# Seven-product gate/up tiles in all four feed-forward blocks instead of two

## The chip, the cores and the metric

The kernel runs on one core of a Trainium2 chip. The metric is the device time of one execution in microseconds (us); lower is better.

## The reference

The program is one inference step of a two-layer decoder for 512 prompt tokens and 64 sample tokens (576 in all, `D_MODEL` 1024), which share their weights. Layer 0 mixes tokens by a recurrence (RWKV-7), layer 1 by dilated window attention. Each layer has a feed-forward block before its mixer and one after it, so that there are four in all. What matters here, cut from the reference:

```python
def swiglu(x, wi, wo):
    gate, up = jnp.split(x @ wi, 2, axis=-1)      # wi: 1024 x 5632, wo: 2816 x 1024
    return (jax.nn.silu(gate) * up) @ wo

h = h + 0.5 * swiglu(rms_norm(h, w['norm_w'][i, 0]), w['ffn1_wi'][i], w['ffn1_wo'][i])
# ... mixer of layer i ...
h = h + 0.5 * swiglu(rms_norm(h, w['norm_w'][i, 2]), w['ffn2_wi'][i], w['ffn2_wo'][i])
h = h + jax.nn.sigmoid(rms_norm(h, w['norm_w'][i, 3]) @ w['pe_gate'][i]) * (p[i] @ w['pe_proj'][i])
```

Between the layers there is also a shared key/value projection, and layer 1 needs a table of position biases.

## The kernel before

Features lie on the 128 partitions and the 576 tokens on the free axis. A matmul streams half of the tokens (288 columns, `HF`) against one 128x128 weight tile. Each float32 operand is split into a high part H (a float32r cast by ACT) and a low part L (the value minus H, by DVE or POOL). A product of two operands is three matmuls, H·H, H·L and L·H. Weights come in pieces of 256 KB on SP's queue (`load_w`, line 166, buffers `wr`); ACT casts them (line 169) and POOL subtracts (line 170).

A feed-forward block (`ffn`) has 22 pairs of a gate tile and an up tile, each of 128 features by 576 tokens, and then the second product with `wo`. Two forms of a pair exist:

- **The standard pair** (`pair`, lines 359 to 373) takes 2 tiles x 8 inner tiles x 3 x 2 halves = 96 matmuls. Its inputs are the split activations `x`. DVE evicts the gate halves (line 365), ACT applies Silu, POOL multiplies by the norm's factor `rs` (line 368), and DVE evicts the up halves (line 371). Then the result `u` is split into two `hv` buffers (lines 154 and 155).
- **The seven-product pair** (`pair7`, lines 375 to 414) regards gate/up by token halves by inner halves as a 2x2 by 2x2 block product, and does it with seven block products (Strassen's scheme in Winograd's form). That is 7 x 4 inner tiles x 3 = 84 matmuls (line 390). Its weights are formed in `seven`: four loads into `wr` and `sr` (line 325), three sums on DVE into PSUM (line 337), one on POOL (line 346), and seven splits (lines 331 and 332). Its token sums are made once a block by `forms`.

`forms` returns five steps. Steps 0 to 3 are `sums(k)`: two normalised activations into two `hv` buffers (line 292), then four sums (lines 294 to 297), split into `TH` and `TL`. Step 4, `quarters`, splits the unsummed parts into the `x` buffers, which are then no longer needed as inputs of standard pairs.

With `fast` given, a block does the first five pairs (`F_STD`) in the standard form, calls step j of `forms` behind pair j, and does the other 17 pairs with seven products. Pair 4 goes through its inner tiles in the outer loop, so that it holds four PSUM banks and releases the `x` buffers one by one. Only the first block of layer 0 ("f0") and the second of layer 1 ("f2") are built with `fast`. The two blocks between them, in phase "f1" (called "f1a" and "f1b" in this text), use 22 standard pairs, two parts of the second product with 11 tiles each, and 26 `hv` buffers. In f1a the three position-bias tables (`bias_table`, called by `mid` behind pairs 2, 5 and 8) are worked in.

The second product is cut into parts, so that `hv` buffers can be used again. A part of tiles a to b starts when pair b (one beyond its last) has been issued (lines 424 to 441).

The order of instructions on each engine's queue is fixed when the kernel is built: a list scheduler takes instructions by program order as priority, and by the times at which its model says that they are ready. On the chip each engine goes through its queue in that order, so that an instruction that waits holds up all those behind it on its engine. Tags such as `hv`, `u`, `t1`, `ev` and `ss` are pools of that many buffers; a new use waits until the last reader of an old one is done.

## Time and profile before

| | us |
|---|---|
| median of 3 runs (lowest to highest) | 2925.57 (2924.57 to 2925.61) |
| the profiled execution | 2930.93 |
| its span, first to last instruction | 2928.8 |
| busy: PE (matmul) | 2786.2, 95% |
| busy: PEld (weight load, beside PE) | 2604.7, 89% |
| busy: DVE / ACT / POOL | 1386.5 / 1198.0 / 1454.0 |

PE runs the matmuls; its busy time is near the span. The profile gives the granted TensorE clock as a share of full speed, 0.975 over the span. Of the blocks named above, f0 takes the time from 8 to 428 us of the span, f1a from 1106 to 1547, f1b from 1629 to 2049, and f2 from 2440 to 2858.

### The profile page before, as it was taken

To read this page: it belongs to the slowest core of one execution; us is meant where nothing else is said; L and a number is where in the kernel's file an instruction comes from. 1 tells how busy PE (TensorE), PEld (TensorE's weight loads), DVE (VectorE), ACT (ScalarE), POOL (GpSimd) and SP (SyncE) were. 2 spreads that over 40 slices of the span, in tenths; PEclk is the share of its full clock that TensorE was granted. 3 is DMA by queue.
4 is the path that set the end of the run, shared out by engine and by line. 5 is a ranking of instruction groups with operands and counts; after the bars stand their busy time and mean duration, and the time that the engine had idled before them with its cause. 6 is when DMAs were issued, how large, how long until landed. Compare 5 with 4: busy or idle time off the path is not lost.

```text
span 2928.8 us, 56127 instructions
## 1 busy us (share of the span) xinstructions
PE 2786.2 (95%) x22360; PEld 2604.7 (89%) x22360; DVE 1386.5 (47%) x2940; ACT 1198.0 (41%) x2296; POOL 1454.0 (50%) x1196
## 2 busy tenths in 40 slices
PE   7899988988999999999999999999999999899997
PEld 7899987977776778999999999999888879899997
DVE  5533338467667654211226321122577775524345
ACT  4434345443333224222335422233456655435354
POOL 6756557553323335444544454454544326757553
PEclk9999998999989899999999999999999999999999
DMA  3233233222113112222233322223433443233223
GB/s 120 81 91 91 87 111 127 70 57 64 44 43 79 40 50 73 85 82 85 83 91 103 96 82 84 83 86 108 131 84 98 132 147 105 80 88 94 87 78 103
DMA packets 177082, 257.81 MB, mean 88 GB/s; under 512 B 46889, under 2 KB 68849, under 8 KB 176820
## 3 DMA queue, kind: packets, MB, share of 16 engines
q1 hardware_dynamic: 148736, 223.56, 25.4%
q10 hardware_dynamic: 28084, 30.66, 3.8%
q8 instruction: 176, 2.88, 0.4%
q14 instruction: 86, 0.70, 0.1%
HBM read 234.31 MB, written 19.85 MB: 87 GB/s over the span
## 4 chain that ended last, share of the span: by engine, by line
PE 71%; DVE 9%; issue 3%; ACT 2%; POOL 2%; DMA 1%; ACTq 0%; DVEq 0%; SPq 0%; POOLq 0%
PE ps_e L196 39%; PE ps_d L517 10%; PE ps_e L390 6%; PE ps_i L517 2%; PE ps_q L517 2%; PE ps_s L517 2%; PE ps_w L517 2%; PE ps_x L517 1%; PE ps_o L517 1%; PE ps_d L390 1%; DVE AR L583 1%; PE ps_pt L526 1%; DVE S L1307 1%; PE ps_d L196 1%; PE ps_y L517 1%
## 5 line engine op out<-in xcount | busy, mean ns | idle before, releaser
L170 POOL TENSOR_TENSOR wl<-wr,wh 128x512 fp32r<-128x512 f32 (+2 forms) x613 | 777.2, 1272 | 975.8 <-ACT wh L169 926.7
L196 PE MATMUL ps_e<-x,wh 128*128 128x288 f32 x3968 | 797.3, 296 | 13.0 <-ACT x L261 7.9
L169 ACT CAST wh<-wr 128x512 fp32r<-128x512 f32 (+2 forms) x613 | 362.2, 594 | 931.7 <-PE ps_e L196 723.8
L196 PEld LDWEIGHTS ps_e<-x,wh 128*128 128x128 f32 x3968 | 639.6, 189 | 18.7 <-ACT x L261 7.9
L196 PE MATMUL ps_e<-hv,wh 128*128 128x288 f32 x2944 | 587.8, 295 | 3.2 <-POOL hv L155 1.9
L196 PE MATMUL ps_e<-x,wl 128*128 128x288 f32 x1984 | 586.5, 296 | 1.4 <-POOL wl L170 1.4
L196 PEld LDWEIGHTS ps_e<-hv,wh 128*128 128x128 f32 x2944 | 472.6, 188 | 4.1 <-POOL hv L155 2.4
L196 PE MATMUL ps_e<-hv,wl 128*128 128x288 f32 x1472 | 434.2, 295 | 1.2 <-POOL wl L170 1.2
L517 PE MATMUL ps_d<-x,wh 128*128 128x288 f32 x1664 | 370.9, 310 | 7.0 <-DVE q L1370 3.3
L196 PEld LDWEIGHTS ps_e<-x,wl 128*128 128x128 f32 x1984 | 373.8, 189 | 2.0 <-POOL wl L170 1.9
L517 PEld LDWEIGHTS ps_d<-x,wh 128*128 128x128 f32 x1664 | 276.1, 192 | 27.5 <-issue 9.3
L196 PEld LDWEIGHTS ps_e<-hv,wl 128*128 128x128 f32 x1472 | 276.8, 188 | 1.5 <-POOL wl L170 1.4
L517 PE MATMUL ps_d<-x,wl 128*128 128x288 f32 x832 | 251.2, 302 | 0.1
L422 DVE SCALAR_TENSOR_TENSOR h<-ps_e,h 128x288 f32<-128x288 f32 x160 | 73.0, 456 | 366.1 <-PE ps_e L196 365.9
L371 DVE TENSOR_TENSOR u<-ps_e,t 128x288 f32<-128x288 f32 x108 | 48.3, 457 | 251.2 <-POOL t L368 142.9
L517 PEld LDWEIGHTS ps_d<-x,wl 128*128 128x128 f32 x832 | 159.9, 192 | 2.2 <-issue 0.5
L365 DVE TENSOR_TENSOR t<-ps_e,rs 128x288 f32<-128x288 f32 x108 | 48.9, 456 | 177.5 <-PE ps_e L196 177.5
L390 PE MATMUL ps_e<-TH,wh 128*128 128x288 f32 x408 | 120.9, 296 | 4.1 <-DVE ev L407 4.0
L390 PE MATMUL ps_e<-TH,wl 128*128 128x288 f32 x408 | 120.3, 295 | 0.0
L390 PE MATMUL ps_e<-TL,wh 128*128 128x288 f32 x408 | 120.2, 295 | 0.0
L1378 POOL TENSOR_TENSOR QS<-q,QS 64x512 fp32r<-64x512 f32 x48 | 63.4, 1321 | 69.2 <-ACT QS L1376 66.6
L332 POOL TENSOR_TENSOR wl<-wr,wh 128x512 fp32r<-128x512 f32 x68 | 88.9, 1310 | 8.7 <-ACT wh L331 5.6
(394 smaller groups left out, 5168.0 us busy)
## 6 DMA issues: line engine op xcount, KB each, us to landing
wr<-in_f1wi SPq DMA_DIRECT2D x142, 256.0 KB
wr<-in_f2wi SPq DMA_DIRECT2D x142, 256.0 KB
wr<-in_f1wo SPq DMA_DIRECT2D x72, 256.0 KB
wr<-in_f2wo SPq DMA_DIRECT2D x72, 256.0 KB
wr<-in_wrkv SPq DMA_DIRECT2D x48, 256.0 KB
wr<-in_wq SPq DMA_DIRECT2D x48, 256.0 KB
sr<-in_f1wi SPq DMA_DIRECT2D x34, 256.0 KB
sr<-in_f2wi SPq DMA_DIRECT2D x34, 256.0 KB
```

Of the source, the lines that this page charges most:

```text
L169: nc.scalar.copy(H, raw)
L170: nc.gpsimd.tensor_tensor(L, raw, H.bitcast(F32), op=ALU.subtract)
L196: nc.tensor.matmul(ps[0:nw], a, b[:, sl], start=k + m == 0, stop=3 * k + m == n - 1)
L332: eng.tensor_tensor(L, a, H.bitcast(F32), op=ALU.subtract)
L365: nc.vector.tensor_tensor(t1[:, sl], ps, rs[:, sl], op=ALU.mult)
L371: nc.vector.tensor_tensor(u[:, sl], ps, t1[:, sl], op=ALU.mult)
L390: nc.tensor.matmul(ps, a, b, start=first and k + m == 0, stop=k == DT // 2 - 1 and m == 2, skip_group_check=True)
L422: nc.vector.scalar_tensor_tensor(h[:, sl], ps, 0.5, h[:, sl], op0=ALU.mult, op1=ALU.add)
L517: self.nc.tensor.matmul(out, lhsT, rhs, **kw)
L526: self.nc.tensor.transpose(out, in_, ident)
L583: nc.vector.scalar_tensor_tensor(m, self.xx[k], self.vec(name, k), self.xn[k], op0=ALU.mult, op1=ALU.add)
L1378: nc.gpsimd.tensor_tensor(qp[H2[1 - par], par], q[o, 0:TP], qp[o, par].bitcast(F32), op=ALU.subtract)
```

## The change

All four blocks are called with `fast`. What follows from that, and goes with it:

- `sums` computes three of the four sums with their splits. The fourth is left unsplit in the second half of buffer `a`, and `quarters` splits it together with the first quarter: eight splits of 576 columns, on DVE and POOL in turn, where there were four of 288 on DVE and four of 576 in turn.
- The steps of `forms` are placed by `STEPS`: step 0 behind pair 0, step 1 behind pair 1, steps 2 and 3 behind pair 2, none behind pair 3, and `quarters` behind pair 4.
- The second product has parts of 7, 7 and 8 tiles in all blocks, and there are 16 `hv` buffers in all blocks.
- Buffers: `t1` 4 everywhere, `ev` 5 instead of 6, `ss` 1 instead of 2. The bias table's one-hot input `oh` is loaded in four pieces of 290 columns into one buffer instead of at once, with four matmuls instead of three; the reversed table goes out in two pieces. `dynamic_dma_scratch_size=1024` is given to the program's builder.

```diff
-N_HF = 18
+N_HF = 16
 N_TF = 3
 F_STD = 5
-F_PARTS = (0, 8, 16, FT)
+STEPS = ((0,), (1,), (2, 3), (), (4,))
+N_S7 = 4
+F_PARTS = (0, 7, 14, FT)
...
             a, b = self.s("hv", self.n_hv), self.s("hv", self.n_hv)
             for t, i in ((a, k), (b, k + DT // 2)):
                 nc.vector.scalar_tensor_tensor(t, self.h[i], self.vec(gain, i), self.rs, op0=ALU.mult, op1=ALU.mult)
-            c, d = self.s("t1", self.n_t1), self.s("u", 2)
+            c, d = self.s("t1", self.n_t1), self.s("u", 2)[:, h0]
             nc.vector.tensor_tensor(c[:, h0], a[:, h1], a[:, h0], op=sub)
             nc.gpsimd.tensor_tensor(c[:, h1], b[:, h1], a[:, h1], op=sub)
-            nc.vector.tensor_tensor(d[:, h0], b[:, h1], c[:, h0], op=sub)
-            nc.gpsimd.tensor_tensor(d[:, h1], b[:, h0], d[:, h0], op=sub)
-            H, L = (self.ph.tile([128, 4, HF], F32R, name=f"T{x}{k}", tag=f"T{x}{k}") for x in "HL")
-            for i, t in enumerate((c, d)):
-                self.split(t.rearrange("p (z t) -> p z t", z=2), H[:, 2 * i:2 * i + 2], L[:, 2 * i:2 * i + 2], (nc.gpsimd, nc.vector)[i])
-            out[k] += [(H[:, i], L[:, i]) for i in range(4)]
+            nc.vector.tensor_tensor(d, b[:, h1], c[:, h0], op=sub)
+            nc.gpsimd.tensor_tensor(a[:, h1], b[:, h0], d, op=sub)
+            H, L = (self.ph.tile([128, 3, HF], F32R, name=f"T{x}{k}", tag=f"T{x}{k}") for x in "HL")
+            self.split(c.rearrange("p (z t) -> p z t", z=2), H[:, 0:2], L[:, 0:2], nc.gpsimd)
+            self.split(d, H[:, 2], L[:, 2])
+            out[k] += [(H[:, i], L[:, i]) for i in range(3)]
             xn.append((a, b))
 
         def quarters():
-            for k in range(DT // 2):
-                H, L = self.xt(k)
-                self.split(xn[k][0][:, h0], H[:, h0], L[:, h0])
-                out[k].append((H[:, h0], L[:, h0]))
-            for k in range(DT // 2):
-                H, L = self.xt(k + DT // 2)
-                self.split(xn[k][1], H, L, (nc.vector, nc.gpsimd)[k % 2])
-                out[k] += [(H[:, h0], L[:, h0]), (H[:, h1], L[:, h1])]
+            for z in range(2):
+                for k in range(DT // 2):
+                    H, L = self.xt(k + z * DT // 2)
+                    self.split(xn[k][z], H, L, (nc.vector, nc.gpsimd)[k % 2])
+                    out[k] += [(H[:, h1], L[:, h1]), (H[:, h0], L[:, h0])] if not z else [(H[:, h0], L[:, h0]), (H[:, h1], L[:, h1])]
...
-        s3 = self.ph.tile([128, n], F32, name="ss", tag="ss", bufs=2)
+        s3 = self.ph.tile([128, n], F32, name="ss", tag="ss", bufs=1)
...
-        self.n_hv, self.n_t1 = (N_HF, N_TF) if fast else (N_HV, 4)
+        self.n_hv, self.n_t1 = N_HF, 4
...
-                return self.ph.tile([128, HF], F32, name="ev", tag="ev", bufs=6)
+                return self.ph.tile([128, HF], F32, name="ev", tag="ev", bufs=5)
...
                     pair(j)
-                    if fast:
-                        steps[j]()
+                    for i in STEPS[j] if fast else ():
+                        steps[i]()
...
-        oh = self.sm("oh", [33, TBW])
-        nc.scalar.dma_start(oh, self.I["onehot"][g])
         tb = self.sm("tb", [16, TBW])
-        for c in range(0, TBW, 387):
-            e = min(c + 387, TBW)
+        for c in range(0, TBW, 290):
+            e = min(c + 290, TBW)
+            oh = self.sm("oh", [33, 290])
+            nc.scalar.dma_start(oh[:, 0:e - c], self.I["onehot"][g][:, c:e])
...
-                self.ffn(I["f2wi"][0], I["f2wo"][0], lambda: self.feed("n03"), self.pre, self.bias_table)
+                self.ffn(I["f2wi"][0], I["f2wo"][0], lambda: self.feed("n03"), self.pre, self.bias_table, fast="n02")
...
-                self.ffn(I["f1wi"][1], I["f1wo"][1], lambda: self.feed("n11", spill=True))
+                self.ffn(I["f1wi"][1], I["f1wo"][1], lambda: self.feed("n11", spill=True), fast="n10")
```

## Rows read from the trace of the kernel before

**Rows 1.** Page, part 4: the chain that ended last, shares by engine.
```profile
PE 71%; DVE 9%; issue 3%; ACT 2%; POOL 2%; DMA 1%; ACTq 0%; DVEq 0%; SPq 0%; POOLq 0%
```

**Rows 2.** Stretches, each start:end us and length, busy us (instructions) per engine, clock, DMA.
```profile
72.00:106.00 34.00, 23.65 (x163) 23.24 (x164) 25.80 (x35) 16.45 (x31) 26.33 (x19) 0.90 0.26 79
2498.60:2530.70 32.10, 21.64 (x141) 21.32 (x140) 22.90 (x30) 15.20 (x29) 24.81 (x19) 0.84 0.24 75
191.60:280.90 89.30, 89.26 (x675) 89.03 (x674) 40.37 (x76) 50.07 (x93) 65.60 (x53) 1.00 0.30 92
1809.00:1900.00 91.00, 91.00 (x689) 91.00 (x688) 14.94 (x27) 22.10 (x37) 43.22 (x34) 1.00 0.29 88
```

**Rows 3.** Chain that ended last, in order of time: start us, us, what.
```profile
431.42 3.12 DMA v<-in_pT
...
683.69 3.86 DMA dE<-Ed
...
2568.91 50.88 PE ps_e L196 x384
...
2638.97 9.54 PE ps_e L390 x72
...
2820.17 1.40 POOL hv L155
```

**Rows 4.** Waits of PE from 2498.6 to 2530.7 us: total us, times, longest.
```profile
PE ps_e L390 <- DVE t L365: 8.5, 1, 8.5
PE ps_e L196 <- DVE u L371: 1.9, 1, 1.9
```

**Rows 5.** Waits of PE from 106 to 428 us.
```profile
PE ps_e L390 <- DVE ev L407: 1.4, 2, 0.9
PE ps_e L196 <- POOL hv L155: 0.9, 1, 0.9
```

**Rows 6.** Waits of PE from 2530.7 to 2858 us.
```profile
PE ps_e L390 <- DVE ev L407: 2.6, 2, 1.5
```

**Rows 7.** Chain that ended last, from 2495 to 2531 us.
```profile
2498.62 1.41 POOL t L368
...
2503.32 3.54 DVE hv L292 x2
...
2506.93 0.95 POOL t L295
...
2510.70 1.60 POOL TL L155
2512.30 0.77 POOL u L297
...
2517.29 2.81 DMA wr<-in_f2wi
...
2520.93 0.37 DVE t L365
```

**Rows 8.** DVE, instructions in order of time; in brackets the idle time before, releaser.
```profile
2513.79 0.76 DVE L155 TENSOR_TENSOR TL<-u,TH 128x576 fp32r<-128x576 f32 x1 [2.78 <-ACT TH L154]
```

**Rows 9.** Stretches of the restart of PE in f2, columns as in Rows 2.
```profile
2521.40:2524.00 2.60, 2.57 (x11) 2.60 (x12) 2.60 (x4) 1.91 (x4) 2.42 (x2) 0.50 0.37 113
2524.00:2527.00 3.00, 3.00 (x14) 3.00 (x14) 2.29 (x5) 1.50 (x3) 3.00 (x4) 0.50 0.00 0
```

**Rows 10.** Groups by line: count | busy us, mean ns | idle before, releasers.
```profile
L155 DVE TENSOR_TENSOR hv<-u,hv 128x576 fp32r<-128x576 f32 x54 | 71.0, 1315 | 37.8 <-ACT hv L154 37.8
L155 POOL TENSOR_TENSOR hv<-u,hv 128x576 fp32r<-128x576 f32 x34 | 48.6, 1428 | 2.4 <-ACT hv L154 2.4
```

**Rows 11.** Lines 292 and 332: count, duration ns min/median/max, first and last start.
```profile
L292 DVE SCALAR_TENSOR_TENSOR hv<-h,vecs,rs x16: 803/806/1850, 37.4 to 2505.0; 128x576 f32<-128x576 f32 x16
...
L332 POOL TENSOR_TENSOR wl<-wr,wh x68: 1272/1296/1802, 87.1 to 2807.9; 128x512 fp32r<-128x512 f32 x68
```

**Rows 12.** Line 1288: the bias table's matmuls.
```profile
L1288 PE MATMUL ps_q<-oh,rb x18: 482/486/496, 1154.8 to 1238.3; 33*16 33x387 f32 x12, 33*16 33x386 f32 x6
```

More of the change, by code (lines that the diff above doesn't have):

```diff
@@ L328, in form @@
         def form(i, a, eng):
-            pool, x, b = (self.ph, "s", 4) if i % 2 else (self.wp, "w", N_W)
+            pool, x, b = (self.ph, "s", N_S7) if i % 2 else (self.wp, "w", N_W)
             H, L = (pool.tile([128, n], F32R, name=x + y, tag=x + y, bufs=b) for y in "hl")
@@ L1281, in bias_table @@
         nc = self.nc
-        oh = self.sm("oh", [33, TBW])
-        nc.scalar.dma_start(oh, self.I["onehot"][g])
         tb = self.sm("tb", [16, TBW])
-        for c in range(0, TBW, 387):
-            e = min(c + 387, TBW)
+        for c in range(0, TBW, 290):
+            e = min(c + 290, TBW)
+            oh = self.sm("oh", [33, 290])
+            nc.scalar.dma_start(oh[:, 0:e - c], self.I["onehot"][g][:, c:e])
             ps = self.bank("q", e - c)
-            nc.tensor.matmul(ps[0:16], self.rb[:, g * 16:(g + 1) * 16], oh[:, c:e], start=True, stop=True)
+            nc.tensor.matmul(ps[0:16], self.rb[:, g * 16:(g + 1) * 16], oh[:, 0:e - c], start=True, stop=True)
             nc.vector.tensor_copy(tb[:, c:e], ps[0:16])
         nc.scalar.dma_start(self.tab[g * 16:(g + 1) * 16], tb)
-        tr = self.sm("tr", [16, SKW])
-        nc.vector.tensor_copy(tr, tb[:, TBW - 1 - SKW:TBW - 1][:, ::-1])
-        nc.scalar.dma_start(self.rev[g * 16:(g + 1) * 16], tr)
+        n = SKW // 2
+        for c in (0, n):
+            tr = self.sm("tr", [16, n])
+            nc.vector.tensor_copy(tr, tb[:, TBW - 1 - c - n:TBW - 1 - c][:, ::-1])
+            nc.scalar.dma_start(self.rev[g * 16:(g + 1) * 16, c:c + n], tr)
     def softmax(self, S, parts, n, adds):
@@ L1789 @@
     arrays = pack(inputs)
-    nc = bacc.Bacc("TRN2", target_bir_lowering=False, num_devices=1)
+    nc = bacc.Bacc("TRN2", target_bir_lowering=False, num_devices=1, dynamic_dma_scratch_size=1024)
     I = {k: nc.dram_tensor("in_" + k, v.shape, mybir.dt.from_np(v.dtype), kind="ExternalInput").ap() for k, v in arrays.items()}
```

## Prediction

> **What bounds the kernel now.** I read the shares of the chain of waits first: PE is 71% of the chain that ended last, and no other engine has more than 9% [rows 1]. So PE's matmuls set the time, and the question is what each stretch of PE costs. Two stretches of the same length show it [rows 2]: in f0, from 191.6 to 280.9 us, seven-product pairs run without a gap, and in f1b, from 1809 to 1900 us, so does the standard work, at 689 matmuls in 91.0 us. The chain in order of time gives the pace of both forms: 384 matmuls of line 196 in 50.88 us and 72 of line 390 in 9.54 us, each 132.5 ns [rows 3]. A matmul costs the same in both forms; only their number differs.
>
> Next I looked where PE does not run at that pace in the two blocks that have seven products already. It is the passage from standard pairs to seven products. Its stretch in f0 is 34.0 us with 163 matmuls, which are worth 21.6 us, so 12.4 us are lost; in f2 it is 32.1 us with 141 matmuls, worth 18.7 us, so 13.4 us are lost [rows 2]. The waits of the latter are one of 8.5 us before the first product, for the gate eviction of pair 4 on DVE (line 365), and one of 1.9 us before pair 4, for the up eviction of pair 3 [rows 4]. After the long wait the granted clock is 0.50 for 5.6 us, the lower level, 1.2 GHz [rows 9]; that is the rest of the loss. The chain in this stretch tells why the eviction, whose data was there since 2512.7 us, came at 2520.9 [rows 7]: two normalisations on DVE take 3.54 us, then POOL makes and splits the sums of step 3, ending with the fourth sum at 2513.07; DVE holds a split of that sum at the head of its queue and idles 2.78 us for it [rows 8]; then come weight sums that wait 2.81 us for a load, and only then line 365. The engine named is DVE, but the cause is an order: the last step of the token sums lies in the last standard pair.
>
> Two small losses recur: PE waits for line 407 behind each of the first two parts of the second product, 1.4 us in f0 and 2.6 us in f2, and 0.9 us for the last `hv` split before the third part [rows 5, 6], which the chain has as 1.40 us of POOL [rows 3].
>
> **Step A, fewer matmuls.** f1a and f1b get 17 seven-product pairs each: 2 x 17 x (96 - 84) = 408 matmuls fewer, at 132.5 ns, −54.1 us, all on PE's path, which has no gap in this stretch of f1b now [rows 2]. What replaces them lies on other engines. POOL, the fullest, is busy 65.6 us in a stretch of 89.3 us (675 matmuls, 8.0 pairs): 8.2 us for each pair of 11.1 us [rows 2], against 73% only. DVE and ACT have 40.4 and 50.1 us there. The loads are four of 256 KB for each pair in both forms.
>
> **Step B, the passage in f0 and f2.** Moving the last sums behind pair 2 takes the POOL chain out of pair 4, and since the fourth sum is no longer split by DVE inside `sums`, DVE's queue no longer holds an instruction that waits for POOL's fourth sum. So the 8.5 us wait should mostly go. What is late next: (1) the wait before pair 4. Two steps of sums now fall into pair 3's 12.7 us. On POOL each is 0.95 + 1.60 + 0.80 = 3.4 us [rows 7], so 3.4 us more than now are ahead of line 368, which releases the up eviction; DVE's own part is free of POOL. I keep 1.9 us. (2) The first product: DVE's and POOL's splits in `quarters` follow pair 4's inner tiles one by one, so at its end one split of 1.3 us on DVE [rows 10] may stand before line 365; 1.3 us. (3) The fourth product needs the splits of the second four quarters, two of them on POOL at 1.43 us each [rows 10] in the fullest stretch; half of that, 1.4 us. (4) 0.6 us for line 407, one wait [rows 5]. No wait is then long enough for the lower clock. Together about 5 us a passage, between 1 us (an eviction and nothing else) and 13.4 us (nothing gained). So B = 2 x 5 − (12.4 + 13.4) = −15.8 us, from −23.8 to +1.
>
> **Step C, the passage in f1a and f1b**, where there was none: 2 x 5 = +10 us, from 2 to 27.
>
> **Step D, the joins in f1.** With three parts these blocks get the waits for line 407 too: as in f0 and f2, 1.4 + 2.6 = +4.0 us, from 0 to 8. In f0 and f2 the parts are 7 instead of 8 tiles, which I cost at nothing: the next pair's loads are behind the same three `wr` buffers.
>
> **Step E, the third part** has 8 tiles instead of 6 in f0 and f2, so 6 more matmuls (0.8 us) run before the last `hv` is wanted: of 0.9 us, 0.1 stay; −1.6 there, +0.2 in f1: −1.4 us, from −1.8 to 0.
>
> **Step F, the bias tables.** The columns are the same, so PE's work is (18 matmuls of 0.486 us before [rows 12], 24 of three quarters of that). But `oh` is one buffer for four loads, so in each of three tables three reloads wait until the matmul before is through. Behind the waiting load on ACT's queue stand the weight casts; behind the waiting matmul on PE stands everything. The trace has no such load; nearest are two waits on ACT's DMAs, 3.12 and 3.86 us [rows 3]. If nothing covered them it would be 9 x 3.86 = 35 us; if other matmuls are ordered in between, 0. The scheduler does order by readiness, and the 2.81 us wait [rows 7] shows that it can be short by a few: I take 4 us, 0.4 a reload.
>
> **At no cost:** 16 `hv` buffers (pairs 0 to 3 and the sums fill them; pair 4's split then waits for the first `quarters`, but is read only by the second product; a part of 7 and one pair ahead are 16; in f1b the key/value projection gives its 16 back before pair 0 ends); `t1` (one more than f0 and f2 had, as many as f1 had); `ev` and `ss` (each pair's are read within that pair, 11.1 us); two more rounds of 16 evictions on DVE, which is under half busy; the smaller DMA scratch. For that the nearest rows are the weight loads, of which a late one costs 2.81 us [rows 7], and I see no reason for a gain or more such waits. The Trainium skill ("SBUF — State Buffer", section "SBUF size: 192, 224, or 256?") has this reserve as the descriptor ring of DMAs issued by GpSimd, of which this kernel has none; no run here shows what it does.
>
> **The sum:** −54.1 − 15.8 + 10 + 4.0 − 1.4 + 4 = −53.3 us. It is made in the profiled execution (2930.93 us, span 2928.8), so 2877.6 us there; that one is 5.4 us above the median of the runs, and 2925.57 − 53.3 = **2872 us**.
>
> **Rivals.** *(1) The passage stays as dear as it is*, since two steps of sums crowd pair 3 and POOL gets four quarter splits instead of two. For it: POOL would have about 12.8 us of work in pair 3's 12.7 us if its weight splits stay; against it: the wait's chain went through a DVE instruction that is gone. Then B is +1, C +27: −54.1 + 1 + 27 + 4 − 1.4 + 4 = −19.5, **2906 us**.
>
> *(2) The one `oh` buffer serialises the tables*, step F at 35 us: −22.3, **2903 us**. It would stand as waits of PE at line 1288 and nowhere else.
>
> *(3) Slower: POOL becomes the bound of f1's seven-product pairs.* A pair's 8.2 us on POOL grow when other engines crowd it; the same weight split takes 1.27 to 1.80 us, and line 292 on DVE 0.80 to 1.85 [rows 11], so there is contention between the two. The gain is gone when 34 pairs lose 53.3 us, 1.57 each: POOL at 12.7 us for a pair, 1.56 times now. At 1.6 times it is 13.1 − 11.1 = 2.0 us x 34 = 67, less 53.3: about **2939 us**. Against it: no row of line 332 is above 1.39 times its median, and f0 runs the same pairs gaplessly. A rule of the Trainium skill ("GPSIMD Engine Reference", section "8. Key points") speaks for this rival: POOL shares its SBUF interfaces with VectorE and contends with DVE instructions with two SBUF inputs. The trace agrees with the contention (1.80 against 1.27 us), not with its being large enough in steady pairs: by the rule at its worst row, 8.2 x 1.39 = 11.4 us a pair, 0.3 us over PE's, the sum would be 34 x 0.3 = 10 us less of a gain.
>
> **How the numbers follow.** What a measurement of this kernel can tell from no change is about 0.2%, 5.9 us. Chances: forecast 0.72 (passages of 1 to 9 us, its own range 2855 to 2892); rival 1 0.14; rival 2 0.07; rival 3 0.04, all slower; and 0.03 that several of these together leave no more than 0.2%. The first three are all faster: 0.93. The low end is the sum with passages of 1 to 2 us and F at nothing, about −70: 2855. The high end takes in the middle of rivals 1 and 2: 2904.
>
> **What would show it.** In the changed profile, line 390 has 68 pairs' matmuls, twice as many, and line 196 has 3264 fewer; a seven-product pair in f1 takes 11.1 us at the same pace. The wait for line 365 before the first product falls from 8.5 to under 3 us in all four blocks, and the granted clock stays at 1.00 there. The wait for line 371 before pair 4 stays near 2 us. Behind two parts in each block there is a wait for line 407 of about 1 us. Waits at the bias table's line sum up to a few us. I am wrong if the wait for line 365 stays above 6 us (rival 1), if PE waits over 10 us for `oh` (rival 2), or if PE waits in every pair of f1 for line 332 on POOL (rival 3).

## The result, and the profile after

The changed kernel takes 2955.03 us (median of 4 runs, 2943.44 to 2961.81), the kernel before in the same comparison 2925.07 us (2921.18 to 2925.61): a ratio of 1.0101, 95% interval 1.0068 to 1.0134. It is slower by 1.0%, where 2872 us were forecast. The profiled execution has a span of 2953.4 us, 24.6 us more than before. The medians differ by 30.0 us, since the profiled execution before was itself 5.9 us above its median; what follows accounts for the 24.6 us of the two traces.

Lines move by one or two in the changed kernel: 196 is now 198, 390 is 389, 365 is 364, 368 is 367, 371 is 370, 407 is 406, 337 is 336, 332 is 331, 1288 is 1287. Two groups of lines from its page, busy time by engine (with instructions) and the shares of the chain that ended last:

```profile
PE 2757.3 (93%) x21958; PEld 2565.7 (87%) x21958; DVE 1528.6 (52%) x3192; ACT 1299.3 (44%) x2532; POOL 1568.7 (53%) x1300
...
PE 70%; DVE 11%; issue 6%; POOL 6%; DMA 4%; ACT 3%; SPq 0%; DVEq 0%; ACTq 0%; POOLq 0%
```

PE has 21958 matmuls, 402 fewer than before (408 fewer in f1, 6 more for the bias tables). So the work went as the change says, and yet DVE, POOL, DMA and "issue" have more of the chain than in [rows 1]. The stretches that answer to [rows 2], the columns as there: the passage in f0 and in f2, then the seven-product pairs between two parts of the second product in f0, f1b and f2.

```profile
70.80:109.00 38.20, 27.60 (x171) 26.52 (x169) 23.06 (x32) 18.27 (x34) 28.96 (x21) 0.87 0.24 76
2510.00:2542.30 32.30, 22.32 (x155) 21.70 (x154) 21.68 (x28) 13.39 (x25) 23.20 (x18) 0.92 0.19 64
177.52:261.91 84.39, 80.25 (x590) 79.64 (x589) 35.40 (x66) 43.18 (x81) 57.74 (x48) 0.98 0.29 90
...
1802.00:1883.91 81.91, 78.81 (x590) 78.03 (x589) 35.44 (x66) 43.00 (x81) 57.70 (x48) 1.00 0.29 90
2623.48:2705.57 82.09, 78.76 (x591) 78.07 (x589) 35.42 (x66) 43.07 (x81) 57.67 (x48) 1.00 0.29 90
```

Seven pairs are 7 x 84 = 588 matmuls, 77.9 us at 132.5 ns (the rows count two or three more at the edges). The three stretches take 84.4, 81.9 and 82.1 us. Before, such a stretch in f0 ran without a gap and f1b's standard work too [rows 2]. I call the length of a stretch less 132.5 ns for each of its matmuls its loss, and every stretch of both executions can be set side by side so:

```
lost by PE, us                                before    after
f0   standard pairs and first sevens           24.3     27.4
     sevens behind the two parts                1.3     13.8
f1a  standard pairs and first sevens           10.1     23.6   (bias tables in it: three before, two after)
     sevens behind the two parts                 -      17.7   (the third table in one)
f1b  standard pairs and first sevens            0       15.5
     sevens behind the two parts                 -      10.5
f2   standard pairs and first sevens           15.6     17.2
     sevens behind the two parts                3.0      8.3
third part of the second product, all blocks    3.6      2.5
```

The losses grow by 136.5 − 57.9 = 78.6 us, the missing matmuls give 402 x 0.1325 = 53.3 us back, and 25.3 us remain, against the span's 24.6. The loss lies in two places: 50.3 − 4.3 = 46 us at the joins (behind the first two parts), and 83.7 − 50.0 = 33.7 us in the passages.

**The joins.** PE's waits in the changed kernel from 133 to 262 us: total us, times, longest.

```profile
PE ps_e L389 <- ACT ev L395: 2.1, 1, 2.1
PE ps_e L389 <- DVE ev L406: 2.1, 1, 2.1
```

The wait for line 406 is the old wait for line 407 [rows 5, 6], longer, and one on ACT's copy (line 395) beside it. The chain that ended last in this place (start us, us, what) and instructions of DVE, ACT and POOL in order of time (in brackets the idle time before, and its releaser) tell what the two wait behind:

```profile
184.25 2.55 POOL wl L331 x2
...
186.81 3.00 DMA wr<-in_f1wi
...
191.23 0.38 DVE ev L406
```

```profile
179.72 0.70 DVE L336 TENSOR_TENSOR ps_q<-sr,wr 128x512 f32<-128x512 f32 x1 [2.98 <-DMA wr<-in_f1wi]
...
189.94 0.70 DVE L336 TENSOR_TENSOR ps_q<-sr,wr 128x512 f32<-128x512 f32 x1 [2.89 <-DMA wr<-in_f1wi]
190.54 0.68 DVE L331 TENSOR_TENSOR sl<-ps_q,sh 128x512 fp32r<-128x512 f32 x1
191.15 0.45 DVE L406 TENSOR_TENSOR ev<-ps_e,ev 128x288 f32<-128x288 f32 x1
```

```profile
180.46 0.59 ACT L330 CAST sh<-ps_q 128x512 fp32r<-128x512 f32 x1 [3.09 <-DVE ps_q L336]
```

```profile
181.64 1.28 POOL L331 TENSOR_TENSOR wl<-ss,wh 128x512 fp32r<-128x512 f32 x1 [5.10 <-ACT wh L330]
```

POOL's last split of a `wr` buffer ends at 186.79, the load of the next weights into it starts at 186.81 and takes 3.00 us, and DVE stands idle for 2.89 us at line 336, the first weight sum of pair 10, while PE is in pair 8. Behind it in DVE's queue is line 406, the eviction of pair 8 that PE needs *now*. The first wait has the same source one load earlier: DVE idles 2.98 us for a load at the sum of pair 9, ACT idles 3.09 us for that sum, and the copy of line 395 comes behind these casts, at 182.50. POOL in turn idles 5.10 us for a cast of ACT, ahead of the splits that free `wr`, so that a late load makes the next one later.

Each load came late because it was asked for late, when a buffer came free. SyncE's queue (start us, us) at the restart of the pairs in f0, the second `wr` load of the second pair behind the part, first of the kernel before, then of the changed one:

```profile
188.34 0.33 SPq L325 DMA_DIRECT2D wr<-in_f1wi  x1
```

```profile
176.57 0.33 SPq L324 DMA_DIRECT2D wr<-in_f1wi  x1
```

PE takes up the pairs at 191.74 us before and at 177.52 us after, so this load leads by 3.4 us before and by 0.95 us after. A part of 7 tiles gives PE 336 matmuls, 44.5 us, a part of 8 gave 384 and 50.9 us [rows 3]; the second product's loads that pass through the same three buffers meanwhile are 16 in both.

**The passage.** PE's waits from 60 to 110 us (f0) and from 2490 to 2550 us (f2), which answer to [rows 4]:

```profile
PE ps_e L198 <- DVE u L370: 4.2, 1, 4.2
PE ps_e L389 <- DVE t L364: 4.2, 1, 4.2
```

```profile
PE ps_e L389 <- DVE t L364: 4.9, 1, 4.9
PE ps_e L198 <- DVE u L370: 4.2, 1, 4.2
```

The 8.5 us before the first product became 4.9, and the 1.9 us before pair 4 became 4.2. The chain through f2's passage shows a cause for each:

```profile
2515.34 1.46 POOL wl L172
2516.80 1.00 POOL t L297
...
2519.03 1.40 POOL TL L157
2520.43 1.44 POOL wl L172
2521.86 1.35 POOL t L367
...
2533.45 1.44 POOL x L157
...
2535.36 1.31 POOL wl L331
...
2536.69 1.20 DMA wr<-in_f2wi
...
2539.64 0.83 DVE ps_q L336
...
2541.71 0.46 DVE t L364
```

Until 2523 us POOL is the one that is late: the second step of sums in pair 3 and two weight splits stand ahead of line 367. After 2533 it looks like the weight supply of the joins: a quarter split (line 157) stands on POOL before the weight split that frees a `wr` buffer, the load follows and lands at 2537.89, and DVE's weight sum starts at 2539.64, behind 1.75 us for which the profile names no releaser (a load of `sr` left behind this one, at 2537.06); line 364 stands behind that sum. The clock answers to [rows 9]: after each wait the granted clock is 0.50 for some microseconds, here behind the second:

```profile
2541.00:2543.00 2.00, 0.69 (x3) 0.72 (x4) 1.90 (x4) 2.00 (x5) 0.76 (x1) 0.50 0.00 0
...
2545.00:2547.00 2.00, 2.00 (x10) 2.00 (x9) 0.00 (x0) 0.92 (x2) 2.00 (x3) 0.50 0.24 72
```

**The bias tables** cost waits on their reloads, from 1129 to 1245 us and from 1245 to 1334 us:

```profile
PE ps_q L1287 <- DMA oh<-in_onehot: 4.0, 3, 1.9
```

```profile
PE ps_q L1287 <- DMA oh<-in_onehot: 3.7, 2, 1.9
```

### The profile page after: what moved, and what is told of

It reads as the page before. It is cut to its first block, busy times and chain, and to the rows that moved or that the text cites. A ratio compares the mean times of both kernels' runs of the same rounds, so it can differ in the third digit from the quotient of the medians.

```text
span 2953.4 us, 56222 instructions
## 1 busy us (share of the span) xinstructions
PE 2757.3 (93%) x21958; PEld 2565.7 (87%) x21958; DVE 1528.6 (52%) x3192; ACT 1299.3 (44%) x2532; POOL 1568.7 (53%) x1300
## 4 chain that ended last, share of the span: by engine, by line
PE 70%; DVE 11%; issue 6%; POOL 6%; DMA 4%; ACT 3%; SPq 0%; DVEq 0%; ACTq 0%; POOLq 0%
PE ps_e L198 25%; PE ps_e L389 20%; PE ps_d L516 9%; PE ps_d L389 3%; PE ps_i L516 2%; PE ps_q L516 2%; PE ps_s L516 2%; PE ps_w L516 2%; POOL wl L172 1%; POOL wl L331 1%; PE ps_x L516 1%; PE ps_o L516 1%; PE ps_d L198 1%; DVE S L1303 1%; PE ps_pt L525 1%
## 5 line engine op out<-in xcount | busy, mean ns | idle before, releaser
L172 POOL TENSOR_TENSOR wl<-wr,wh 128x512 fp32r<-128x512 f32 (+2 forms) x477 | 598.9, 1265 | 694.4 <-ACT wh L171 653.9
L171 ACT CAST wh<-wr 128x512 fp32r<-128x512 f32 (+2 forms) x477 | 277.1, 586 | 573.6 <-PE ps_e L198 298.0
L198 PE MATMUL ps_e<-x,wh 128*128 128x288 f32 x1792 | 371.0, 302 | 25.3 <-DVE u L370 12.8
L198 PEld LDWEIGHTS ps_e<-x,wh 128*128 128x128 f32 x1792 | 296.3, 193 | 30.3 <-issue 15.2
L198 PE MATMUL ps_e<-x,wl 128*128 128x288 f32 x896 | 268.4, 300 | 1.6 <-POOL wl L172 1.6
L389 PE MATMUL ps_e<-x,wh 128*128 128x288 f32 x1088 | 230.2, 305 | 31.5 <-DVE ev L406 18.4
L389 PEld LDWEIGHTS ps_e<-x,wh 128*128 128x128 f32 x1088 | 180.8, 195 | 37.0 <-DVE ev L406 21.4
L331 POOL TENSOR_TENSOR wl<-wr,wh 128x512 fp32r<-128x512 f32 x136 | 177.8, 1310 | 11.1 <-ACT wh L330 9.9
L330 ACT CAST sh<-ps_q 128x512 fp32r<-128x512 f32 x136 | 79.9, 588 | 222.3 <-DVE ps_q L336 184.7
L331 POOL TENSOR_TENSOR wl<-ss,wh 128x512 fp32r<-128x512 f32 x68 | 88.6, 1302 | 166.4 <-ACT wh L330 156.4
L198 PEld LDWEIGHTS ps_e<-x,wl 128*128 128x128 f32 x896 | 172.4, 193 | 2.1 <-POOL wl L172 2.0
L389 PE MATMUL ps_e<-x,wl 128*128 128x288 f32 x544 | 164.8, 303 | 0.0
L331 DVE TENSOR_TENSOR wl<-ps_q,wh 128x512 fp32r<-128x512 f32 x68 | 47.0, 691 | 222.2 <-ACT wh L330 222.2
```

The costliest lines, as they stand in the source:

```text
L171: nc.scalar.copy(H, raw)
L172: nc.gpsimd.tensor_tensor(L, raw, H.bitcast(F32), op=ALU.subtract)
L198: nc.tensor.matmul(ps[0:nw], a, b[:, sl], start=k + m == 0, stop=3 * k + m == n - 1)
L330: nc.scalar.copy(H, a)
L331: eng.tensor_tensor(L, a, H.bitcast(F32), op=ALU.subtract)
L389: nc.tensor.matmul(ps, a, b, start=first and k + m == 0, stop=k == DT // 2 - 1 and m == 2, skip_group_check=True)
```

## The experiments

Losses are those of the one profiled execution, ratios go against the kernel before. The scheduler orders all queues anew for each of these kernels, so an edit can act through an order that it did not name. Two theories stood at the start: the raw-weight supply through three buffers runs dry (shorter parts, one `ss` buffer), or the new order of the token sums and the quarters is at fault.

**e1, the kernel before with the parts of the change.**
```
-F_PARTS = (0, 8, 16, FT)
+F_PARTS = (0, 7, 14, FT)
```


> The kernel before with one edit: second product in parts of 7, 7 and 8 tiles instead of 8, 8 and 6, in f0 and f2. Theory 1 (supply: while the last tiles of a part run on PE, the weights of the next seven-product pairs have to be loaded and formed, and a part of 7 tiles leaves 0.8 us less for each output tile; the waits for the first pair behind a part then grow from 0.2 to 1.6 us each to about 4 us or more): f0 and f2 lose about 18 us less 1.6 us won at the third part, so 2938 to 2943 us. Theory 2 (the single ss buffer makes the joins dear): no change, 2924 to 2926 us. Theory 3 (it is the moved token sums that make later pairs late): no change, 2924 to 2926 us.

2929.77 us, ratio 1.0020 [1.0005, 1.0034]. The four stretches behind a part lose 4.06, 3.59, 3.52 and 3.76 us (before 0.22, 1.08, 1.71, 1.32), 10.6 us more together, and the medians differ by 5.9 us. PE's waits from 125 to 300 us, where the kernel before has none in f0's first such stretch:

```profile
PE ps_e L390 <- ACT ev L396: 1.9, 1, 1.9
PE ps_e L390 <- DVE ev L407: 1.7, 1, 1.7
```

The same two waits as after, made by the shorter part alone. The second `wr` load of the second pair behind the first part in f0 leaves at 172.77 us, 0.99 us ahead of the restart at 173.76, as late as in the changed kernel:

```profile
172.77 0.33 SPq L325 DMA_DIRECT2D wr<-in_f1wi  x1
```

The cost is well under the 18 us that were expected, and the interval leaves out, narrowly, the "no change" of the other two theories. So "parts of 7 at nothing" was wrong.

**e2, the kernel before with one `ss` buffer.**
```
-        s3 = self.ph.tile([128, n], F32, name="ss", tag="ss", bufs=2)
+        s3 = self.ph.tile([128, n], F32, name="ss", tag="ss", bufs=1)
```


> The kernel before with one edit: one buffer ss instead of two for the weight sum of POOL, in f0 and f2. Theory 1 (parts of 7): no change, within 2 us of 2925. Theory 2 (a single ss makes POOL's sum for the next pair wait for the split of the last one, and the first pair behind each part is late by it): 18 us more in f0 and f2, about 2943 us.

2929.31 us, ratio 1.0024 [1.0009, 1.0040]. The first sevens lose 5.69 and 5.25 us (before 2.34, 2.79), the first stretch behind a part in f0 3.88 (before 0.22). Some of it is only moved: the other three stretches lose 1.6 us less together and the standard pairs 0.4 and 1.5 us less, so that about 6 us are left (5.4 in the medians). Less than expected, but not nothing: `ss` was costed at nothing too. At the restart in f0 POOL makes pair 10's sum into `ss` at 195.54 us, ahead of two splits that free `wr` (196.79); with two buffers it had started that sum at 184.52. The changed kernel's POOL has the same order (183.00 and 184.25). So a single `ss` holds up the splits that free `wr` by one sum; that this is all of its effect is not shown.

**e3, the changed kernel with one step of sums behind each of the first four pairs.**
```
-STEPS = ((0,), (1,), (2, 3), (), (4,))
+STEPS = ((0,), (1,), (2,), (3,), (4,))
```


> The changed kernel with one edit: the token sums behind pairs 0, 1, 2 and 3 again, one step each. Theory 3 (two steps in pair 3 crowd POOL, and that is why the passage costs 15 to 16 us instead of 5): the wait for line 370 before pair 4 falls from 4.2 to about 2 us and the passages together get 20 to 40 us shorter, 2915 to 2935 us. Theory 4 (the restart is set by the weights of the first seven-product pairs, whose sums stand on DVE ahead of the gate eviction and wait for loads, wherever the token sums are): waits move between pair 4 and the first product, the total stays within 8 us of 2955.

2950.02 us, ratio 1.0098 [1.0074, 1.0123]; standard pairs and first sevens lose 24.8, 13.2 and 15.1 us in f0, f1b and f2 (changed kernel 27.4, 15.5, 17.2). PE's waits from 60 to 110 us:

```profile
PE ps_e L389 <- DVE t L364: 7.9, 1, 7.9
PE ps_e L198 <- DVE u L370: 1.1, 1, 1.1
```

The wait before pair 4 falls to 1.1 us, and the one before the first product is nearly as long as that of [rows 4]. The doubled step sets *where* PE waits and hardly how long.

**e4, the changed kernel with one load of `oh` for each table** (all pieces of a table use its first columns, so the tables' values are others).
```
-            oh = self.sm("oh", [33, 290])
-            nc.scalar.dma_start(oh[:, 0:e - c], self.I["onehot"][g][:, c:e])
+            if not c:
+                oh = self.sm("oh", [33, 290])
+                nc.scalar.dma_start(oh, self.I["onehot"][g][:, 0:290])
```


> The changed kernel, but each bias table loads its one-hot input once (the first 290 columns) and uses it for all four matmuls, so the nine reloads are left out and the tables' contents are not the reference's. If the reloads are what makes the tables dear (PE waits of 7.7 us for the load and 2.1 us for the copy in the trace, and the lower clock behind them): 12 to 20 us less, 2935 to 2943 us. If the weights' supply is the bound there anyway: less than 6 us, 2949 to 2955 us.

2936.14 us, ratio 1.0044 [1.0029, 1.0059]; the stretches of f1a with tables lose 16.4 and 8.7 us instead of 23.6 and 11.6. Ten microseconds of the trace hang on the reloads, more than the waits named `oh` add up to (7.7), so that other waits hang on them too. By the medians it is 19 us; the profiled execution, 2949.38 us, was the slowest of nine.

**e5, the changed kernel with an order:** the first weight sum of a pair goes behind the eviction `c22` (line 406) of the pair before it, in DVE's queue, without a wait.
```
-        s1 = diff(raw["21"], raw["22"], ALU.add)
+        s1 = diff(raw["21"], raw["22"], ALU.add, self.c22)   # ordered behind c22 of the pair before
```


> The changed kernel with one edit: the first weight sum of a seven-product pair is ordered behind the eviction c22 (line 406) of the pair before it, on the same engine, DVE. Theory 4 (what PE waits for is an eviction that stands on DVE behind a weight sum of a later pair, which itself waits for a load): the waits for line 364 before the first product (4.2 us in f0, 4.0 in f1b) and for line 406 behind the parts (2.0 to 3.3 us) go, with the lower clock behind the former; 5 us in each of four passages and 2 us at each of eight joins, some 30 us less: 2920 to 2930 us. Rival (the weights themselves are late, so PE then waits for the weight splits instead): within 8 us of 2955, with waits for lines 330 and 331 in place of those for 364 and 406.

2934.67 us, ratio 1.0034 [1.0019, 1.0048], 20 us less than the changed kernel. The passages of f0, f1b and f2 lose some 4 us less (f0 19.95 instead of 24.05 before the first product, f1b 8.13 instead of 12.24, f2 9.83 instead of 13.86); f0's joins fall from 6.5 and 7.3 to 3.9 and 4.0, those of f2 stay at 4.1; f1a's stretches with tables lose 3.4 us more. What the joins still lose is no wait at the restart: in f0 PE now waits for ACT's copy (line 398) once in each of six pairs, 2.4 us in all. So the sum that stands ahead of the evictions is one part of the cost, but not the root, and holding it back has a price of its own.

**e6, the same order in the kernel before.**

> The kernel before with the same one edit of order. Theory 4: the wait of 8.5 us for line 365 in f0 and f2 falls to about 4, and the waits for line 407 (1.4 and 2.6 us) go: 8 to 14 us less, 2910 to 2917 us. Rival (weights late): within 4 us of 2925.

2947.55 us, ratio 1.0077 [1.0051, 1.0103]: a clear miss. PE's waits in the pairs from 194.3 to 292.6 us:

```profile
PE ps_e L393 <- ACT ev L399: 7.5, 7, 1.4
```

Once in each of seven pairs, where the kernel before had no wait. ACT idles for the held-back sum (4.64 us before 216.48) and then does its casts in a row ahead of the copy that PE waits for. The order of DVE's queue is no fault in itself; while the loads are in time, the early sum is what keeps PE fed.

**e7, the changed kernel with a fourth raw-weight buffer.** To make room, the bias table is stored in its four pieces as they come (`tb` 290 columns instead of all). The line below is changed so at three places.
```
-            raw = self.wp.tile([128, c * nw], F32, name="wr", tag="wr", bufs=N_W - 1)
+            raw = self.wp.tile([128, c * nw], F32, name="wr", tag="wr", bufs=N_W)
```


> The changed kernel with four buffers wr for raw weights instead of three (room for it is made by storing the bias table in four pieces). If the supply of raw weights bounds joins and passages: waits of DVE for wr loads shrink, the joins lose 1 to 2 us instead of 4 to 7, 20 to 30 us less in all, 2925 to 2935 us. If POOL's and ACT's forming of the weights bounds them, or the order on DVE alone: less than 8 us, 2947 to 2957 us.

2900.03 us, ratio 0.9912 [0.9886, 0.9938], 55 us less than the changed kernel and about twice what was expected. The first stretches behind a part in f0 and f1b, and the load that left 0.95 us ahead of the restart in the changed kernel:

```profile
173.63:251.49 77.86, 77.86 (x591) 77.86 (x590) 32.56 (x62) 42.18 (x79) 56.84 (x48) 1.00 0.29 90
1771.90:1849.88 77.98, 77.98 (x591) 77.98 (x590) 32.16 (x61) 42.15 (x79) 56.85 (x48) 1.00 0.29 90
```

```profile
168.47 0.33 SPq L324 DMA_DIRECT2D wr<-in_f1wi  x1
```

PE is busy for the whole of each, with no gap, and the same holds for the second stretches, for f2 and for f1a's stretch without a table. All seven joins without a table are free: of the 54 us by which this trace is shorter, some 41 are the joins'. The load leads by 5.16 us (the restart is at 173.63). POOL is as busy as it was (56.8 of 77.9 us). The passage keeps most of its loss: 24.7 us in f0, 13.3 in f1b and 14.9 in f2, some 2.4 us less each. In f0 the wait for line 364 is gone, and there are two for line 370:

```profile
PE ps_e L198 <- DVE u L370: 7.3, 2, 4.2
```

**e10, the kernel before with the fourth buffer,** which needs the smaller DMA scratch of the change for room.

> The kernel before with four buffers wr (and the smaller DMA scratch, which makes the room). If the raw weights' supply sets its joins and the restart in f0 and f2: the joins' 4.3 us go, and the wait of 8.5 us for line 365 shrinks to under 4: 10 to 16 us less, 2909 to 2915 us. If the supply was bound by it in parts of 7 alone: the joins' 4 us at most, 2921 to 2925 us.

2919.64 us, ratio 0.9992 [0.9980, 1.0005]: no difference that this measurement tells. Its stretches behind a part lose −0.08 to 0.07 us (before 4.3 in all), its passages as much as ever (24.8 and 16.1 us). In the kernel before three buffers were nearly enough. The smaller scratch, tried only together with the buffer, does no harm that shows.

**e8, the changed kernel with the order of e5, the spread steps of e3, two `ss` and three `oh` buffers.**

> The changed kernel with four edits that the earlier runs point to: order as in the run before last but two, token sums one step behind each of pairs 0 to 3, two buffers ss, and three buffers oh with the bias table stored in pieces. If the effects add up (order 30, spread 5, ss 10, reloads 15 us): about 2895 us, below the kernel before. If order does nothing: about 2925 us.

2962.31 us, ratio 1.0130 [1.0101, 1.0159]: a miss by some 65 us and the slowest of all, with 6.9 to 7.7 us lost at each join without a table, where e5 had 4. In f0's first join that is the wait of e6: 5.9 us for ACT's copy in six pairs, up to 1.4 us each, where e5 had 0.4. e6 and e8 have the order with two `ss` buffers, e5 with one; which edit does it was not tried. With three raw buffers these repairs don't add up.

**e9, e11, e12, the changed kernel with four `wr`, three `oh` buffers and the order of the passage varied:** the spread steps of e3 (e9); these and the first sevens' first weight sum ordered behind pair 3's last up eviction, "gate" (e11); the steps of the change, with the gate (e12).
```
+                if j == F_STD - 2:
+                    self.gate = i          # pair 3's up eviction; the next s1 is ordered behind it
```


> The changed kernel with four buffers wr, the token sums one step behind each of pairs 0 to 3, and three buffers oh. With raw weights no longer short, the place of the sums should count: Theory 5 (two steps in pair 3 crowd POOL, and the wait of 4.2 us for line 370 before pair 4 in the run with four wr is that): the loss from pair 0 to the first part falls from about 14 us in f1b to 8 to 10, and the reloads of oh cost 3 to 6 us less in f1a: 2900 less 20 to 26, 2875 to 2880 us. Rival (sums' place does not matter either way, as with three wr): only the reloads' 3 to 6 us, 2894 to 2897 us.

> As the run with four wr, spread sums and three oh, and also: the first weight sum of pair 5 is ordered on DVE behind the last up eviction of pair 3 (line 370), which it preceded. Theory 4 (a weight sum that waits for its load holds up the eviction behind it: 1.7 us of DVE idle and 3.5 us of PE before pair 4): 2 to 4 us less in each of four passages, 8 to 16 us below that run, about 2865 us. Rival: the passage is bound by POOL, and the order changes less than 4 us.

> As the run before it, but with the token sums as in the change (two steps behind pair 2). If two steps in pair 3 crowd POOL and delay line 367 (t x rs), which the last up eviction waits for: 4.2 us of wait for line 370 in each passage stay, 8 to 16 us above the run before it. If the order on DVE was the cause: within 4 us of it.

2887.54 (0.9886 [0.9863, 0.9908]), 2889.66 (0.9882 [0.9863, 0.9902]) and 2882.04 us (0.9864 [0.9850, 0.9879]). PE's waits from 60 to 110 us, in e11 and in e12 (where lines 367 and 373 are the changed kernel's 364 and 370):

```profile
PE ps_e L394 <- DVE t L367: 6.8, 1, 6.8
PE ps_e L198 <- DVE u L373: 1.6, 1, 1.6
```

```profile
PE ps_e L198 <- DVE u L373: 4.2, 1, 4.2
```

The three have f1b's passage at 11.8, 9.9 and 10.0 us. e9 lies between its two expectations. e11 misses the first of its by 25 us and is as its rival has it: what the gate takes from one wait stands in the next. e12 is 7.6 us below e11, which neither of its expectations has, but the intervals of the two overlap.

**e13, e12 with pair 3's product `t1` x `rs` (line 367 of the changed kernel) on DVE instead of POOL.**
```
-                    nc.gpsimd.tensor_tensor(t1, t1, rs, op=ALU.mult)
+                    (nc.vector if fast and j == F_STD - 2 else nc.gpsimd).tensor_tensor(t1, t1, rs, op=ALU.mult)
```


> As the last run (four wr, three oh, gate order, sums as in the change), and the product of t and rs of pair 3 (line 367 of the changed kernel) is done by DVE instead of POOL, in all four blocks. Theory 5 (PE's wait of 4.2 us before pair 4 is POOL's queue: two steps of sums and two weight splits stand ahead of this product): the wait falls below 1.5 us, the lower clock behind it goes, 4 to 6 us less in each of four passages: 2882 less 16 to 24, 2858 to 2866 us. Rival (the up eviction is late for DVE's own queue or for Silu on ACT): within 5 us of 2882, with another name at the same wait.

2888.03 us, ratio 0.9882 [0.9868, 0.9897], and the wait for line 373 goes from 4.2 to 3.6 us only. POOL's queue ahead of that one instruction is not the cause by itself: in f1b DVE has a split of the token sums ahead of the product (1.36 us) and takes 1.75 us for it.

**e14, e12 with the bias tables behind pairs 0, 1 and 2** instead of 2, 5 and 8, so none stands among seven-product pairs; **e15, e13 and e14 together.**
```
-                if mid and j in (2, 5, 8):
-                    mid(j // 3)
+                if mid and j < 3:
+                    mid(j)
```


> As the last run, with the bias tables behind pairs 0, 1 and 2 of f1a instead of 2, 5 and 8, so that none is among seven-product pairs. If the tables cost there because their matmuls' PSUM banks and copies are shared with the weight sums (PE then waits 3.2 and 3.1 us for line 330 and falls to the lower clock): the losses of 9.5 and 8.0 us in f1a's first two stretches of seven products fall to about 2.3 and 0.1, less 3 us for the two tables' own matmuls elsewhere: 10 to 13 us less, 2869 to 2872 us. If their price is the matmuls and loads wherever they stand: within 4 us of 2882.

> Both edits of the two runs before. If both theories hold the gains add: 26 to 37 us less than 2882, 2845 to 2856 us. If the passage's floor is elsewhere, only the tables' part is left, about 2870 us.

2874.17 us (0.9835 [0.9819, 0.9852]) and 2873.99 us (0.9833 [0.9819, 0.9848]): the tables' place is worth 8 us, and pair 3's product on DVE nothing, with the tables early either. f1a's stretches of sevens lose 1.4, 0.4 and 0.4 us; in e12 PE had waited there for weights behind the tables, from 1183 to 1310 us:

```profile
PE ps_e L394 <- ACT sh L330: 6.4, 2, 3.2
```

**e16, e17, e14 with the doubled step behind pair 0 and behind pair 1.** In e14 the stretch before pair 4 and the one behind it, up to the first product, are:

```profile
65.30:76.30 11.00, 5.48 (x40) 5.04 (x38) 7.95 (x9) 3.70 (x8) 10.54 (x9) 0.88 0.13 43
76.30:90.40 14.10, 14.05 (x90) 13.86 (x91) 13.25 (x16) 9.10 (x15) 11.41 (x9) 0.85 0.29 99
```

```
e16: STEPS = ((0, 1), (2,), (3,), (), (4,))      e17: STEPS = ((0,), (1, 2), (3,), (), (4,))
```


> This is e14's kernel with the two steps of token sums that share one pair put behind the first standard pair instead of the third: steps 0 and 1 behind pair 0, 2 behind pair 1, 3 behind pair 2, the quarters behind pair 4 as before. Theory 6: what is left of the passage in e14 comes from two steps of sums within one pair's time, which fill POOL when that pair is late: from 65.3 to 76.3 us POOL is busy 10.54 of 11.00 us with line 370 behind the sums, and PE waits 4.2 us for line 373; from 27 to 40 us, after pair 0, POOL is busy 5.41 of 13.00 us, so two steps (about 3.4 us each on POOL) fit there. By it the wait for line 373 before pair 4 falls under 1 us in all four blocks, no wait of more than 1 us for an eviction comes in its place, the clock stays up, and about 7 us a block come back: 2874 - 4 x 7 = 2846, between 2840 and 2856. Rival 6a: the passage's cost is the whole work that DVE and POOL have to do before the first product (sums, quarters, the seven weights), wherever it lies; then a wait of about 4 us appears at another eviction (pair 2's, or line 367's of pair 4) and the time stays within 6 us of 2874. Rival 6b: two steps so early hold back the rest of pair 0 and 1 (the rms scale comes late, DVE is busy 11.90 of 12.00 us from 15 to 27): slower than 2880.

> As e16, with the two steps behind the second standard pair: step 0 behind pair 0, 1 and 2 behind pair 1, 3 behind pair 2. Theory 6 has POOL busy 9.66 of 12.60 us from 40 to 52.6 us with one step, so a second one (3.4 us) fills it as it fills the pair after now: the wait for line 373 moves one pair ahead, with 2 to 4 us, and the time lies between e16's and e14's, 2850 to 2872. Rival 6a: within 6 us of 2874.

2875.58 us (0.9824 [0.9807, 0.9840]) and 2876.33 us (0.9826 [0.9810, 0.9842]), no other than e14. PE's waits of e16 from 15 to 110 us:

```profile
PE ps_e L198 <- ACT TH L156: 3.1, 1, 3.1
PE ps_e L198 <- DVE x L264: 2.7, 2, 2.5
PE ps_e L394 <- DVE t L367: 2.2, 1, 2.2
PE ps_e L198 <- DVE u L373: 1.7, 1, 1.7
```

The wait for line 373 falls from 4.2 to 1.7 us, as the theory of the doubled step has it, and 3.1 us for a split of a token sum and 2.2 us for the gate eviction come in its place, as its rival has it; the passages still lose 10.2 us in f1b (e14 10.4). Theory 6 fell. In the two rows above, the 25 us before the first product, DVE is busy 21.2 us and POOL 22.0 us. That fits a passage whose price is the whole work that these two must do before the first product, but what is shown is only that seven arrangements with four raw buffers (e7, e9, e11, e12, e14, e16, e17) cost 9.9 to 13.3 us in f1b, the five with the gate 9.9 to 10.4; taking work out of the passage was not tried, so its floor stays open.

## Why the prediction was wrong, step by step

The chance of "slower" was put at 0.04, and it is slower. By the steps:

- **A** (−54.1): right. −53.3 us with the tables' six matmuls, and the pace in stretches without a wait is 132.5 ns as before.
- **D and "at no cost"** (joins in f1 +4.0, parts of 7 "at nothing", one `ss` at nothing): this is the step that failed. The joins cost 13.8 − 1.3 + 8.3 − 3.0 = 17.8 us more in f0 and f2, 10.5 us in f1b and 17.7 us in f1a, of which up to 11.6 stand at a table. I wrote of the parts that "the next pair's loads are behind the same three `wr` buffers", and took it as a reason for no change. It was the reason for the loss: those buffers also carry the second product's weights, and a part that is 6.4 us shorter takes the lead of the second pair's last `wr` load from 3.4 to 0.95 us. The 2.81 us wait for a load of `wr` in [rows 7] could have been read as a sign that the supply had little to spare. e1 and e2 show each of the two edits doing some harm alone (5.9 and 5.4 us by the medians), e1 with the same short lead (0.99 us), and e7 shows the cause: with one more buffer the lead is 5.16 us and all joins without a table are free.
- **B** (−15.8): +4.7. Of its four terms, (1) was mis-sized against its own working: 3.4 us more of POOL's work ahead of line 368 were counted and 1.9 us kept; 4.2 us came in f0, f1b and f2 each. (2) was 1.3 us; it became 4.0 to 4.9 us there, by late weights as far as the chain tells, which the step did not look at; four raw buffers took this wait away in f0 and yet gave back only some 2.4 us a passage (e7), so what sets the passage's price stays open. (4)'s 0.6 us is not in [rows 5], which have 0.9 and 0.5; it changes nothing. The lower clock, counted out for want of a long wait, stayed.
- **C** (+10): with 15.5 us in f1b, and f1a's put at as much (its table can't be told apart), some 31 us, by the same waits. That is above its upper bound of 27.
- **E** (−1.4): −1.1 us, right: third parts lose 0.6 us in each block.
- **F** (+4): too small. There are five waits for `oh`, 7.7 us. f1a lost 15.3 us more than f1b where the tables of before had lost 10.1 (a table's matmuls are longer than 132.5 ns in both), which leaves 5.2 us; but without the reloads (e4) the stretches with tables lose 10 us less, and the median is 19 us lower.

Summed up by these: −53.3 + 4.7 + 31 + 17.8 + 21 (joins of f1, without the tables' part, put at f1b's 10.5 in both) − 1.1 + 5.2 = 25.3 us. This closes on the losses by its making, as F is put at what f1a has left over. Of the rivals, (1) was true of the passages, but says nothing of the joins. (2) was a part, 5 to 10 us of the traces instead of its 35. (3) named the wrong resource: PE waits for no weight split on POOL in steady pairs, and line 331 on POOL has the median of 1296 ns that line 332 had [rows 11]. The rule of the Trainium skill beside it ("GPSIMD Engine Reference", section "8. Key points", on the SBUF interfaces that POOL shares with VectorE) was put at 10 us of lost gain in steady pairs at its worst; no such loss is seen there in e7's stretches without a gap. The rival I lacked was the slow one that happened: a supply that was just enough, asked for a little more.

The forecast's number itself is what the kernel gives once the supply is mended: e14 has 2874 us, with four `wr` buffers, three for `oh`, the gate and the tables early. That is chance and no credit to the working, since e14's passages still cost twice what I allowed (10.4 us in f1b against 5).

## What to carry to other kernels

A change of tile counts is a change of prefetch lead: before "the same buffers" is costed at nothing, read on the load queue how long ahead of its use each load is issued, and what the shorter stretch leaves of that. In an in-order engine queue an instruction for later work that waits for a load holds up the eviction for present work, so the page names the evicting engine where a DMA is at fault; a fourth raw buffer mended that here (55 us), while moving the instruction back helped where the loads were late and cost where they were not (e5 gained 20 us, e6 lost 22). Where several placements of the same work give the same time within a few microseconds, suspect that the place of the wait is not its cause.

## What the runs showed of the hardware

After waits of 4 to 5 us, TensorE's granted clock stands at 0.50, the 1.2 GHz level, for some microseconds (rows of 2541 to 2547 us above), so a wait of 4.2 us before pair 4 costs more than itself: the 90 matmuls behind it took 149 instead of 132.5 ns each, 1.5 us. Shorter waits can do the same, and do not always. Behind the second waits of the first joins in f0 and f1b, the clock (the third number from the end) was:

```profile
191.65:195.55 3.90, 3.90 (x18) 3.90 (x19) 1.97 (x4) 1.65 (x3) 1.35 (x3) 0.56 0.22 67
1814.90:1818.00 3.10, 2.95 (x22) 2.95 (x23) 2.12 (x5) 1.74 (x3) 1.52 (x3) 1.00 0.29 85
```

In f0 PE had waited 2.1 us twice, 6.5 us of work apart, and a matmul then took 240 ns for 3.9 us; in f1b it had waited 1.1 and 2.0 us, and the clock stayed up. The means over the whole stretches, 0.98 and 1.00, hide this. Of the 6.5 us that f0's first join lost, some 2 us are the lower clock, not the waits.
